# A hybrid encoder layer on one core: a new order of instructions and a new assignment of buffers, which count on the landing of stores

## The chip, the cores and the metric

One core of a Trainium2 chip runs the whole layer in one launch. The time is in device microseconds, the median of three runs. The engines are named as in the profile: PE (TensorE matmuls) and PEld (its weight loads), DVE (VectorE), ACT (ScalarE), POOL (GpSimd) and SP (SyncE, which here only issues DMAs).

## The reference

One layer on 512 tokens of width 1024, in f32:

```
h = rmsnorm(x) ; p = h @ w_in                      # 1024 -> 9248 columns
rx, ry, qkv, z, ba, gates = split(p)
y_rnn = rglru(conv4(rx), gelu(ry)) @ w_rnn_proj    # 12 blocks of 128, forward and backward scan
y_dn  = deltanet(silu(conv4(qkv)), z, ba) @ w_dn_proj   # 8 heads, chunks of 64, two directions
x = x + (sigmoid(g1) * y_rnn + sigmoid(g2) * y_dn) @ w_out
gt, up = split(rmsnorm(x) @ w_gate_up)             # 1024 -> 2 x 2816
x = x + (silu(gt) * up) @ w_down
out = rmsnorm(x)
```

## The kernel before

Large products are made in three parts: each f32 operand is split into a rounded fp32r part (`hi`, an ACT cast) and the rest (`lo`, a DVE subtraction), and PE adds hi·hi, hi·lo and lo·hi, 128x512 or 128x256 at a time. Most of the large products are also done with seven block products in place of eight (`merged`, `products`, `gate_up`, `down_first`, `down_second`), whose sums of weight blocks are made ahead of time. The small products (transposes, the deltanet's 128x128 state, its triangular inverse) are plain f32.

The program runs in this order: the norm and transposition of x; four groups of rglru blocks (`rg_group`), with the first deltanet front (`dn_front`) and the z product (`zset`) between; the rnn projection (`rset`); for each of four pairs of heads `dn_mats`, `dn_inverse`, `dn_state`, `dn_out`, interleaved with the next front and with steps of the two gate products; the deltanet and output projections; the FFN. Weights come by SP's DMA queue, mostly 512 KB to a transfer; some are added up in place by POOL's.

Five intermediate results go out to DRAM and come back, and the stores lie on SP's queue like the loads: `gcr` (the deltanet's cumulated decays; it comes back broadcast to all partitions in `dn_mats`), `xqd` (sums of blocks of the normalized x), `zs` (silu of z), `osums` (sums of blocks of w_out, stored by `out_sums`, 512 KB to a store, two stores for each of four j) and `sums` (the same for w_down). `kept` is a small sixth.

No statement of the kernel runs where it is written. Each engine call is recorded (`Rec`), and `Plan.emit` (lines 491 to 511) issues the 9344 recorded calls in the order of a table of numbers, `ORDER`. A second table, `HOMES`, gives each of 1930 tiles of the groups `t2` (2 KB a partition), `t4` (4 KB a partition) and `ps` (a PSUM bank) the number of the buffer it lives in. Every line of the profile is L525 for that reason, and the tile names carry the meaning: `t4788` is the 788th tile, from group `t4`. Both tables come out of a planner that is not part of the kernel. What the chip must wait for is added when the calls are issued: `emit` has the first writer of a reused buffer wait for its last users on other engines,

```
for other, last in before[home].items():
    if other != eng:
        self.tc.add_manual_dep(ins, last.name, info, reason="the buffer's last use")
```

and a load by SP into a buffer that an SP store is reading waits besides for the landing of that store, although both are on one queue: a DMA only reads its source after it was issued. That wait stands in the built program whatever the planner thinks of it. SP takes its instructions in order, so whatever stands behind a waiting load waits with it.

Each DMA of SP and ACT reports its landing on one of eight semaphores, DMAHW0 to DMAHW7, taken in turn. A DMA therefore also waits for the landing of the one that had its semaphore before it, eight DMAs back (in the rows below: the one DMAHW that goes up by one from row to row).

Of the kernel before, what the change touches and what calls it, by code (L numbers as in the profile page):

```python
# [31 lines left out]
11 0 2 1685 1686 10 14 3 5 7 1 151 152 154 70 9 1703 12 13 140 1687 153 1689 143 1688 1690 65 17 18 19 20 21 22 23  # L32
24 25 26 27 34 36 28 29 30 15 16 35 33 31 32 41 44 42 37 39 43 38 45 66 1697 1691 1692 47 1704 1723 1698 51 49 50 71
1705 1706 53 67 68 72 40 73 1707 1708 59 74 1741 1724 57 1693 1694 1699 1700 1701 1695 77 234 1742 97 96 158 52 69
46 1696 1702 58 75 54 55 78 56 76 1725 1726 48 79 80 81 89 1727 1728 1743 1744 88 60 93 63 64 1715 1709 84 61 82
1716 1717 1718 1710 62 90 85 1729 1735 83 1719 1720 1745 1746 1711 1712 1713 1714 1736 1737 1730 1738 1739 1740 92
1731 1732 1733 1734 1747 1748 1753 1754 104 99 1749 1755 1721 105 106 100 1756 107 1750 1751 135 109 133 1752 98 159
160 1757 101 86 119 117 102 103 1758 1722 116 108 91 94 126 134 125 87 127 132 95 312 390 155 1763 110 313 235 144
118 111 112 236 124 130 113 314 122 161 1759 120 128 138 162 163 164 165 166 167 168 169 170 171 172 315 316 139 237
238 239 317 318 319 320 240 241 242 243 244 245 246 247 248 249 250 251 252 253 254 255 256 257 258 259 260 261 262  # L40
321 322 323 363 364 324 325 326 327 328 329 330 331 332 333 334 136 335 129 336 131 114 1764 123 121 137 263 115 6
337 338 339 340 341 342 343 344 345 346 365 264 265 266 267 268 269 270 271 272 273 173 1760 753 347 1111 1080 1081
1762 754 756 174 175 1112 1113 176 177 757 391 178 147 142 141 146 157 145 149 216 274 275 276 277 179 156 762 278
279 280 180 181 182 183 184 148 185 767 150 418 186 187 188 189 190 191 281 282 283 284 192 348 349 350 351 352 3931
609 353 354 355 356 357 358 359 360 286 855 285 287 856 909 5682 289 193 361 288 362 196 665 666 417 582 636 857 290
392 1761 203 195 197 367 194 528 291 1235 198 368 419 583 292 369 293 199 637 370 1766 910 294 371 393 638 394 395
396 397 398 399 400 401 402 403 404 405 406 407 408 409 410 411 412 413 414 415 416 200 366 529 204 421 205 206 372
422 303 1173 858 859 8 207 423 4804 304 299 208 295 296 297 298 4805 305 306 860 861 862 474 424 425 300 301 530 381
373 374 307 308 210 302 863 375 426 309 310 211 584 531 532 533 376 311 780 209 420 427 385 386 387 388 1765 475
1236 777 534 212 779 435 436 377 378 379 380 864 865 866 867 868 869 870 871 382 383 882 883 1021 213 778 214 781  # L50
786 791 439 440 441 872 873 874 875 876 877 878 879 880 881 431 432 215 433 384 389 758 760 442 434 796 218 535 428
429 536 768 770 437 763 585 430 886 438 782 759 219 448 1114 610 1115 586 764 1116 449 476 587 443 787 588 887 537
538 539 540 1117 541 542 543 544 545 546 1118 1119 765 1237 1120 453 884 547 788 548 549 755 888 783 1174 589 590
591 592 593 594 595 596 597 598 599 600 601 451 992 550 551 766 602 603 445 552 553 554 667 559 792 889 890 604 605
606 607 608 444 560 772 1121 1122 784 1175 761 502 790 1083 1084 1085 1086 1087 1088 1123 1124 1125 1126 1127 1128
1129 1130 1131 1132 1133 1134 1135 1136 1082 789 911 1089 1090 556 501 455 896 1137 785 561 450 885 562 1091 1092
1093 1094 1095 1096 904 769 771 1097 1098 1099 1100 1101 1102 1103 891 452 454 1104 1105 468 469 892 613 614 1106
797 799 477 462 463 1022 1023 478 479 480 481 482 905 900 901 893 902 897 898 483 484 485 486 487 488 489 490 491
492 493 494 495 496 456 615 616 1107 1108 1138 611 612 1142 903 617 894 464 1024 1025 828 555 899 794 793 795 912
497 498 499 500 895 906 557 1109 563 1110 1238 1239 1240 1241 1242 1243 564 465 913 558 505 506 1026 907 937 908  # L60
1139 773 775 936 565 566 774 776 1244 1140 507 1027 1028 1141 618 470 508 1055 1057 446 503 1029 1030 1031 1032 1033
1034 1245 1246 1247 1248 1249 1250 914 1035 1036 915 1054 1056 1251 1252 1253 1254 1255 1256 1257 1258 1259 1260
1261 4896 1037 1038 1039 1040 577 578 801 447 457 1041 569 1042 993 471 573 1266 1043 1044 1045 1046 472 619 620 621
570 571 574 575 1068 1069 509 802 567 568 916 917 918 919 920 921 201 1047 922 923 924 925 1070 504 926 1262 927 928
929 930 931 932 933 934 576 579 935 511 515 510 512 963 513 572 1176 1177 1072 938 622 516 1178 517 514 1263 580 518
940 829 466 723 1143 631 623 632 633 804 805 806 807 202 1071 994 1073 634 624 625 626 627 628 629 630 467 1179 1180
1181 1182 1183 1184 1185 1186 995 725 458 1279 941 1187 731 724 808 809 1188 1189 810 581 728 732 1190 1191 1192
1193 1194 1195 811 812 1196 1197 1373 1198 1199 1264 942 939 803 813 814 815 816 817 818 819 820 821 822 459 823 824
830 1200 825 831 826 730 827 996 997 998 999 1000 1001 1002 964 943 944 950 954 832 1003 1004 1204 217 1005 1006
1007 1008 1009 1010 1011 1012 1013 1014 1015 1201 1265 946 1202 1016 1282 833 1017 1018 733 727 729 945 947 951 952  # L70
955 948 956 726 734 834 635 1203 668 669 670 671 672 673 460 674 675 676 677 678 679 473 741 747 680 1205 835 958
959 960 836 735 4822 681 682 683 684 742 953 685 686 949 687 688 689 690 957 639 694 640 519 641 520 691 521 642 643
1283 1145 1146 961 798 800 748 523 524 525 644 645 1147 1286 461 646 647 648 649 650 522 850 651 695 652 653 654
1148 655 656 657 1149 743 749 744 751 745 736 1150 1151 658 659 660 661 662 1152 962 1319 526 842 1269 527 4861 837
843 844 851 852 1374 1019 846 847 848 692 1207 1048 228 227 663 1320 750 1281 4823 746 737 853 752 1144 1208 1209
1210 1211 1212 1213 1214 1215 1216 1217 1218 1219 1220 838 839 840 4789 1206 1375 738 229 1321 965 4824 4825 230
2374 849 1059 1221 1222 1223 1224 1225 1226 1227 1228 1229 1230 1153 1154 1155 1156 1157 1158 1159 1160 841 845 739
1061 1231 1232 664 4806 1051 1053 4856 4807 1427 1058 1233 1060 854 231 693 1050 1052 2393 232 1272 1234 966 967 968
969 970 1271 1161 1162 1163 1164 1165 1166 1167 1168 2367 1169 2400 1454 1062 1270 1074 4 2394 1170 1171 1376 1377
1378 1379 1380 1381 1382 1383 1384 1385 1386 1387 1388 1389 1390 1391 971 972 1273 1063 1280 1284 1392 1393 1394  # L80
1395 1268 1075 1396 1397 1398 1399 220 233 1428 973 974 975 976 977 978 979 980 981 982 983 984 985 1274 1172 1267
1400 1401 1076 1077 1285 223 1287 1078 1346 1064 4839 696 1296 1404 1298 4838 4860 1275 1276 1277 1278 1300 1405
1406 1049 1290 224 2397 1402 2395 1656 2368 2371 2372 2375 2401 986 2370 2379 2378 1322 2369 987 988 4857 1407 1408
1065 1020 1323 1324 1325 1326 2382 989 2377 221 222 1327 1328 1329 1330 1331 1332 1333 1334 1335 1336 1337 1338 1339
1340 1341 1342 1343 1344 1345 1350 1351 1352 1353 1066 1067 1657 1409 740 4788 2376 1455 4790 2380 2373 225 1403
1288 697 698 699 700 4840 990 701 702 703 704 705 706 707 708 709 710 711 712 713 1297 1301 1429 714 1430 1347 1289
1291 1293 1294 1295 1292 991 715 716 717 718 719 720 721 1658 4791 1305 1431 1432 1433 1456 722 1418 1419 1354 1422
1299 1303 1348 1302 2917 1306 2381 2387 4928 1420 1423 1424 1425 1355 1457 1349 4874 1421 1426 2365 2386 2384 2385
1410 2366 1411 1412 1414 1415 1416 1417 1413 1434 1435 1436 1437 1438 1439 1440 1441 1442 1443 1444 1445 1573 1446
# [1925 lines left out]
```

## Time and profile before

| | us |
|---|---|
| median of 3 runs (lowest, highest) | 1043.67 (1043.47, 1044.1) |
| the profiled execution, its own time | 1040.58 |
| its span, first to last instruction | 1038.9 |
| PE busy in the span | 1022.7 |
| DVE busy | 946.1 |
| ACT busy | 749.8 |
| POOL busy | 121.1 |

The profiled execution is 3.09 us faster than the median of the timed runs. In the rows that follow, a busy time is the time in which the engine had at least one instruction under way; on PE the ends of matmuls are modelled and overlap, so a matmul's price is the distance from its start to the next one's. "x" counts instructions. In a row of the waits, the engine that waited stands ahead of the arrow and what released it behind.

### The profile page before, as it was taken

The page shows a single profiled execution, that of the slowest core. Times are in us where ns is not written, and L with a number is a line of the kernel's source. Part 1 is how long each engine was busy: PE and PEld are TensorE (multiplying, and loading weights), DVE is VectorE, ACT ScalarE, POOL GpSimd, SP SyncE. Part 2 cuts the span into 40 slices and gives each one's busy share as a digit, 9 for nine tenths or more (in the row PEclk, how much of TensorE's full clock was granted, in tenths as well). Part 3 has the DMA queues.
Part 4 walks back from the last instruction along what each step waited for, and adds up shares of the span by engine and source line. Part 5 has one row for each costly group of instructions (what it writes and reads, how often), then busy time and mean ns, then how long its engine had stood idle before and what let it go on. Part 6 is the DMA issues. An engine that isn't in the chain of part 4 may idle for free. (4 is left out here: it accounts for less than half of the span.)

```text
span 1038.9 us, 18186 instructions
## 1 busy us (share of the span) xinstructions
PE 1022.7 (98%) x6623; PEld 888.7 (86%) x6623; DVE 946.1 (91%) x1707; ACT 749.8 (72%) x1384; POOL 121.1 (12%) x165
## 2 busy tenths in 40 slices
PE   9999999999999998999999999999999999999997
PEld 8888888888888886879878888889999999998886
DVE  6999999998778888979999988999999899999997
ACT  7899999986674577798887585778454555556664
POOL 6000001220012216221322000000000000000000
PEclk9999999999999999999999999999999999999999
DMA  9954236796678789995966745961575643155632
GB/s 301 272 162 132 67 100 185 181 248 166 177 199 185 168 243 284 222 264 172 260 138 154 216 123 186 289 174 62 173 224 173 207 149 102 42 160 191 236 103 82
DMA packets 170873, 186.30 MB, mean 179 GB/s; under 512 B 8704, under 2 KB 120464, under 8 KB 170784
## 3 DMA queue, kind: packets, MB, share of 16 engines
q1 hardware_dynamic: 157648, 156.43, 48.5%
q0 software_dynamic: 11808, 25.30, 14.4%
q10 hardware_dynamic: 1328, 3.42, 0.9%
q8 instruction: 52, 0.85, 0.3%
q14 instruction: 37, 0.30, 0.1%
HBM read 159.92 MB, written 18.91 MB: 172 GB/s over the span
## 5 line engine op out<-in xcount | busy, mean ns | idle before, releaser
L525 DVE TENSOR_TENSOR t<-t,t 128x1024 fp32r<-128x1024 f32 (+14 forms) x839 | 550.7, 685 | 37.4 <-ACT t L525 17.8
L525 PE MATMUL ps<-t,t 128*128 128x512 f32 (+3 forms) x3195 | 574.9, 328 | 5.3 <-DVE t L525 2.3
L525 PEld LDWEIGHTS ps<-t,t 128*128 128x128 f32 (+1 forms) x3195 | 454.8, 180 | 70.8 <-DVE t L525 4.4
L525 ACT CAST t<-t 128x1024 fp32r<-128x1024 f32 (+2 forms) x418 | 323.2, 808 | 128.6 <-PE ps L525 64.0
L525 PE MATMUL ps<-hh,t 128*128 128x512 f32 (+2 forms) x1424 | 369.7, 340 | 0.3 <-ACT t L525 0.3
L525 PEld LDWEIGHTS ps<-hh,t 128*128 128x128 f32 (+1 forms) x1424 | 247.1, 189 | 29.5 <-ACT t L525 0.7
L525 PE MATMUL ps<-hl,t 128*128 128x512 f32 (+2 forms) x720 | 230.7, 339 | 0.0
L525 PEld LDWEIGHTS ps<-hl,t 128*128 128x128 f32 (+1 forms) x720 | 134.4, 189 | 14.3
L525 ACT COPY t<-ps 128x256 f32<-128x256 f32 (+3 forms) x168 | 69.9, 434 | 62.4 <-PE ps L525 53.1
L525 ACT ACTIVATE t<-t 128x128 f32<-128x128 f32 (+5 forms) x118 | 71.8, 618 | 19.0 <-DVE t L525 14.7
L525 DVE SCALAR_TENSOR_TENSOR t<-ps,par,t 128x511 f32<-128x511 f32 (+1 forms) x108 | 79.0, 745 | 6.8 <-ACT t L525 5.8
L525 ACT ACT_TABLE_LOAD x56 | 71.8, 1283 | 4.4 <-issue 1.9
L525 DVE TENSOR_TENSOR t<-ps,t 128x256 f32<-128x256 f32 (+1 forms) x102 | 53.3, 528 | 8.4 <-PE ps L525 5.7
L525 DVE TENSOR_TENSOR t<-t 128x512 f32<-128x512 f32 (+1 forms) x84 | 53.4, 643 | 2.8 <-PE ps L525 2.3
L525 PEld LDWEIGHTS ps<-t,na 128*128 128x128 f32 (+2 forms) x640 | 43.7, 146 | 7.4 <-issue 3.2
L525 PE MATMUL ps<-t,na 128*128 128x128 f32 (+2 forms) x640 | 49.0, 233 | 0.9 <-DVE t L525 0.6
L525 ACT ACTIVATE t<-ps,par 128x512 f32<-128x512 f32 x68 | 45.4, 707 | 4.2 <-PE ps L525 3.9
L525 POOL TENSOR_SCALAR_AFFINE_SELECT t<-t 128x512 f32<-128x512 f32 x32 | 25.9, 864 | 184.8 <-ACT t L525 153.9
L525 PE MATMUL ps<-ident,t 128*128 128x128 f32 (+1 forms) x232 | 44.5, 274 | 1.2 <-ACT t L525 0.5
L525 POOL DMA_DIRECT2D t<-in_w_in_dram x24 | 31.1, 1364 | 73.4 <-DVE t L525 39.6
L525 PEld LDWEIGHTS ps<-ident,t 128*128 128x128 f32 (+1 forms) x232 | 29.2, 141 | 7.9 <-ACT t L525 1.5
L525 ACT ACTIVATE t<-ps 128x256 f32<-128x256 f32 (+1 forms) x46 | 21.8, 486 | 16.3 <-PE ps L525 15.9
(153 smaller groups left out, 683.5 us busy)
## 6 DMA issues: line engine op xcount, KB each, us to landing
t<-in_w_in_dram SPq DMA_DIRECT2D x66, 512.0 KB, 5.4
t<-in_w_gate_up_dram SPq DMA_DIRECT2D x44, 512.0 KB, 4.7
t<-xqd SPq DMA_DIRECT2D x48, 256.0 KB, 4.9
t<-in_w_in_dram POOLq DMA_DIRECT2D x24, 512.0 KB, 7.5
t<-in_w_down_dram SPq DMA_DIRECT2D x22, 512.0 KB, 4.4
t<-in_w_down_dram SPq DMA_DIRECT2D x33, 256.0 KB, 4.1
t<-in_w_in_dram SPq DMA_DIRECT2D x24, 256.0 KB, 4.2
t<-in_w_out_dram SPq DMA_DIRECT2D x12, 512.0 KB, 5.3
```

What stands on the lines that cost most here:

```text
L525: self.plan.ops.append((self.eng, {x.tensor.name for x in aps}, outs, lambda: real(*a, **kw)))
```

## The change

Nearly all of `ORDER` and of `HOMES` is new: 1788 of the 1930 buffer numbers differ, and a call stands on average 28 places (of 9344) from where it stood, at most 702. The code, the operations, their shapes and the DMAs are the same; only what the engines do next, and where tiles lie, is changed. The planner that wrote the tables counts a wait that it had not counted: a load into a buffer that a store of the same queue reads waits for that store's landing. The core of the diff:

```
 ORDER = """
-11 0 2 1685 1686 10 14 3 5 7 1 151 152 154 70 9 1703 12 13 140 1687 153 1689 143 1688 1690 65 17 18 19 20 21 22 23
...
+11 0 2 1685 1686 10 14 1 3 5 7 151 140 152 153 154 70 143 1687 1688 1689 1690 65 17 18 19 20 21 22 23 24 25 36 26 27
...
 HOMES = """
-1 3 0 4 2 0 4 9 5 15 1 3 6 7 6 7 2 8 9 2 10 11 14 12 13 13 12 25 23 15 22 20 6 3 7 1 5 0 14 24 5 12 7 5 5 0 5 0 10 2
...
+1 5 0 7 2 0 3 8 4 13 1 3 6 7 4 6 3 8 9 0 10 11 12 13 14 18 17 27 24 15 26 23 6 5 1 3 2 2 19 25 7 9 1 14 0 10 0 6 12
...
```

What that does is seen in the instructions of an engine in their order. The first place is SP's queue in `out_sums` and `dn_mats` of the second pair of heads, in the profile of before at 382 to 394 us. `osums<-t4911` and `osums<-t4910` are the two stores of one j; `t4788` and `t4784` receive the broadcast decays; `t4476` is a block of gate weights. Before:

```order
L525 DMA osums912_989<-t4911_988 128x1024 [waits DMAHW4_49,DVE_49]
L525 DMA t4788_865<-gcr100_177 128x4x128 [waits DMAHW4_49,DMAHW5_49,DVE_49,PE_49]
L525 DMA t4784_861<-gcr100_177 128x4x128 [waits DMAHW6_49,PE_49]
L525 DMA osums912_989<-t4910_987 128x1024 [waits DMAHW7_49,DVE_49]
L525 DMA t4476_553<-in_w_in_dram 128x2x512 [waits DMAHW7_49,DMAHW0_49]
L525 DMA t4471_548<-in_w_in_dram 128x2x512 [waits DMAHW1_49,DMASW5_49,DVE_49]
L525 DMA t4488_565<-in_w_in_dram 128x2x512 [waits DMAHW2_49,DMASW7_49,PE_49]
```

After:

```order
L525 DMA osums912_989<-t4911_988 128x1024 [waits DMAHW2_49,DVE_49]
L525 DMA t2475_552<-xqd112_189 128x512 [waits DMAHW3_49,PE_49]
L525 DMA osums912_989<-t4910_987 128x1024 [waits DMAHW7_49,DMAHW4_49,DVE_49]
L525 DMA t4788_865<-gcr100_177 128x4x128 [waits DMAHW5_49,DMASW2_49,DVE_49]
L525 DMA t4784_861<-gcr100_177 128x4x128 [waits DMAHW6_49,PE_49]
L525 DMA t4476_553<-in_w_in_dram 128x2x512 [waits PE_49]
L525 DMA t2474_551<-xqd112_189 128x512 [waits DMAHW0_49]
L525 DMA t4865_942<-in_w_in_dram 128x8x128 [waits DMAHW1_49,PE_49]
```

Before, the store of `t4911` reports on DMAHW4 and the next load waits for DMAHW4, because `t4788` lies in the buffer of `t4911`; the store of `t4910` reports on DMAHW7 and the load of `t4476`, into the buffer of `t4910`, waits for it. After, the four tiles lie elsewhere, and no row behind the two stores (they report on DMAHW2 and DMAHW4) waits for them.

Over the whole queue: of the seven loads or stores behind an `osums` store that waited for its landing within three rows, one is left (`t4608`, a block of w_rnn_proj, behind the store of `t4922`); of the loads that wait for the landing of a `sums` store at most three rows ahead there were two, and there are three.

The second place is PE at the start, where the transposes of the second half of x (`ident`, f32) meet the first z products (fp32r, into ps458 and ps459). Before:

```order
L525 MATMUL ps458_535<-t4464_541,t424_101 128x512
L525 MATMUL ps65_142<-ident1_78,t457_134 128x128
L525 MATMUL ps62_139<-ident1_78,t457_134 128x128
L525 MATMUL ps65_142<-ident1_78,t457_134 128x128
L525 MATMUL ps458_535<-t4464_541,t424_101 128x512
L525 MATMUL ps459_536<-t4464_541,t424_101 128x512
L525 MATMUL ps63_140<-ident1_78,t457_134 128x128 x2
L525 MATMUL ps459_536<-t4464_541,t424_101 128x512
L525 MATMUL ps63_140<-ident1_78,t450_127 128x128
```

After:

```order
L525 MATMUL ps459_536<-t4464_541,t424_101 128x512 x2
L525 MATMUL ps64_141<-ident1_78,t457_134 128x128
L525 MATMUL ps65_142<-ident1_78,t457_134 128x128
L525 MATMUL ps62_139<-ident1_78,t457_134 128x128
L525 MATMUL ps63_140<-ident1_78,t457_134 128x128
L525 MATMUL ps62_139<-ident1_78,t457_134 128x128
L525 MATMUL ps65_142<-ident1_78,t457_134 128x128
L525 MATMUL ps63_140<-ident1_78,t457_134 128x128
L525 MATMUL ps64_141<-ident1_78,t457_134 128x128
```

The f32 transposes stand together, where before PE went back to fp32r twice among them. Over the whole order PE goes from an f32 matmul to an fp32r matmul 169 times before and 158 times after. ACT's order has 61 table loads where it had 56; every other instruction is there as often as before.

876 rows, old and new, of tables (HOMES, ORDER) are left out of this document.

## Prediction

> **What bounds the kernel now.** I read the page's shares first, then a table of stages, then PE's waits, then SP's, and last the two places where PE stood still longest.
>
> The page's first line for PE:
>
> ```profile
> PE 1022.7 (98%) x6623; PEld 888.7 (86%) x6623; DVE 946.1 (91%) x1707; ACT 749.8 (72%) x1384; POOL 121.1 (12%) x165
> ```
>
> PE is without work for 1038.9 - 1022.7 = 16.2 us of the span, and the change leaves each of its matmuls in place. Where those 16.2 us lie is seen in the stretches of time (length, then busy time and count of PE, PEld, DVE, ACT and POOL, PE's clock, share of the DMA engines, GB/s):
>
> ```profile
> 0.00:52.00 52.00, 49.39 (x301) 43.39 (x302) 42.12 (x89) 43.94 (x81) 17.57 (x29) 1.00 0.99 286
> 52.00:160.00 108.00, 108.00 (x480) 88.64 (x481) 106.03 (x132) 105.05 (x148) 0.00 (x0) 1.00 0.39 120
> 160.00:385.00 225.00, 225.00 (x1278) 187.07 (x1276) 192.16 (x314) 163.37 (x273) 42.80 (x48) 1.00 0.79 196
> 385.00:415.00 30.00, 26.73 (x122) 20.92 (x120) 26.06 (x45) 21.30 (x60) 16.73 (x24) 1.00 0.88 258
> 415.00:530.00 115.00, 114.70 (x792) 95.07 (x791) 103.50 (x262) 98.81 (x214) 28.42 (x40) 1.00 0.85 213
> 530.00:545.00 15.00, 13.33 (x256) 9.89 (x255) 14.67 (x24) 12.62 (x26) 6.20 (x7) 1.00 0.87 198
> 545.00:700.00 155.00, 153.27 (x1045) 130.47 (x1046) 143.48 (x329) 109.54 (x223) 9.36 (x19) 1.00 0.66 191
> 700.00:1020.00 320.00, 319.88 (x2301) 303.12 (x2300) 304.88 (x489) 187.17 (x345) 0.00 (x0) 1.00 0.47 148
> 1020.00:1038.90 18.90, 12.35 (x61) 10.11 (x59) 13.22 (x31) 7.99 (x20) 0.00 (x0) 0.93 0.31 112
> ```
>
> PE's idle time by stage is length less busy: 2.61 at the start, 0.00 from 52 to 385, 3.27 in the thirty microseconds from 385, then 0.30, 1.67, 1.73, 0.12, and 6.55 at the end. Start and end are the first loads and the last norm, whose rows stand nearly as they did. So a new order can win at most 3.27 + 0.30 + 1.67 + 1.73 + 0.12 = 7.1 us there, 0.7%, and 3.27 of it lies in one place.
>
> The place is where SP waits for stores. SP's own waits for the landing of a store (total, times, longest):
>
> ```profile
> SPq L525 <- DMA osums<-t: 31.8, 7, 7.2
> SPq L525 <- DMA xqd<-t: 5.8, 3, 3.7
> SPq L525 <- DMA zs<-t: 5.8, 2, 5.1
> SPq L525 <- DMA sums<-t: 4.1, 2, 2.7
> ```
>
> That is 47.5 us in which nothing else went out on that queue. Most of it cost PE nothing, as the stages without idle time show. From 380 to 394 two stores follow each other; SP's issues there:
>
> ```profile
> 382.64 0.32 SPq L525 DMA_DIRECT2D osums<-t  x1
> 386.28 0.92 SPq L525 DMA_DIRECT2D t<-gcr  x2
> 387.30 0.45 SPq L525 DMA_DIRECT2D osums<-t  x1
> 392.66 1.91 SPq L525 DMA_DIRECT2D t<-in_w_in_dram  x4
> ```
>
> and its waits for stores in that window:
>
> ```profile
> SPq L525 <- DMA osums<-t: 8.0, 2, 4.8
> ```
>
> The gcr loads go out 3.64 us after the first store and the four w_in loads 5.36 us after the second, 8.0 us of it waiting. Meanwhile the DMA engines run dry and are then flooded, in 40 slices of 0.75 us from 385 to 415 (tenths of busy share, then GB/s):
>
> ```profile
> DMA  3004689840055999999999999999999999999999
> GB/s 126 0 0 147 151 222 358 323 175 22 0 41 137 350 410 404 399 393 327 293 339 388 382 265 210 238 254 262 270 265 256 225 197 259 334 379 378 393 423 333
> ```
>
> What hangs on those loads, in order of time (start, length, in brackets the idle time before and its releaser):
>
> ```profile
> 390.71 4.00 POOL L525 TENSOR_SCALAR_AFFINE_SELECT t<-t 128x512 f32<-128x512 f32 x4 [3.43 <-DVE t L525]
> 391.38 2.04 ACT L525 ACTIVATE t<-t,ngc 128x128 f32<-128x128 f32 x6 [2.74 <-POOL t L525]
> 397.28 1.22 POOL L525 DMA_DIRECT2D t<-in_w_in_dram  x1 [2.57 <-DVE na L525]
> 398.02 1.14 POOL L525 TENSOR_SCALAR_AFFINE_SELECT t<-t 128x512 f32<-128x512 f32 x1
> 399.20 0.88 DVE L525 SCALAR_TENSOR_TENSOR na<-ps,dns,t 128x256 f32<-128x256 f32 x2 [2.03 <-POOL t L525]
> 402.65 0.96 PE L525 MATMUL ps<-t,t 128*128 128x512 f32 x3 [2.06 <-DVE t L525]
> 411.55 1.05 ACT L525 CAST t<-t 128x1024 fp32r<-128x1024 f32 x1 [1.85 <-DMA t<-in_w_in_dram]
> 413.73 0.50 PE L525 MATMUL ps<-t,t 128*128 128x512 f32 x1 [1.19 <-ACT ps L525]
> ```
>
> And the landings of the gcr loads from 385 to 415 (count, size, median us from issue):
>
> ```profile
> t<-gcr SPq DMA_DIRECT2D x2, 256.0 KB, 4.4
> ```
>
> 386.28 + 4.4 is 390.7, the moment at which POOL starts: POOL masks the decays that gcr brought, ACT takes their exp, POOL masks again, and only then can DVE write `na`; its 2.03 us of waiting pass on to PE as 2.06. Then ACT stands 1.85 us for a w_in load and PE 1.19 for ACT. I read both of PE's waits, 2.06 + 1.19 = 3.25 of the 3.27, as the late tail of these two stores.
>
> **The change part by part.**
>
> *Stores waited for.* The order shows that neither the gcr loads nor the w_in loads behind these stores wait for them any more. Removed are up to 3.64 and 5.36 us of SP. What that is worth to PE is bounded above by the stage's idle time, 3.27, and by what DVE has to spare there, 30.00 - 26.06 = 3.94; below by nothing (a loss is the second rival). I take 3.27, since the chain leads from the store to both waits without a break. What is late next is the ordinary run of the neighbouring stages: from 415 to 700 PE is idle 0.30 + 1.67 + 1.73 = 3.70 us in 285, so 0.4 in 30. Net -2.9. The other osums, xqd, zs and sums waits count nothing: PE's own work hides them, and if that cover went they would cost what the covered places do not cost now.
>
> [...]
>
> *Fewer changes of precision on PE.* Of the 169 places where PE goes from f32 to fp32r, 11 are gone. Their price:
>
> ```profile
> 405.19 0.48 PE L525 MATMUL ps<-hh,t 128*128 128x512 f32 x1
> 405.51 0.39 PE L525 MATMUL ps<-hl,t 128*128 128x512 f32 x1
> 405.74 0.40 PE L525 MATMUL ps<-hh,t 128*128 128x512 f32 x1
> ```
>
> The first comes straight behind transposes and takes 405.51 - 405.19 = 0.32 us to the next start; the second takes 0.23. So 0.09 each, 11 x 0.09 = 1.0 us, on PE itself and hence on the path. Its bounds are 0 (four of the 11 are at the start, where PE waits for loads anyway) and 1.0; I take -1.0, as the rest of PE's time has no holes to hide it.
>
> *Five more table loads on ACT.* Each as on the page:
>
> ```profile
> L525 ACT ACT_TABLE_LOAD x56 | 71.8, 1283 | 4.4 <-issue 1.9
> ```
>
> 5 x 1.28 = 6.4 us on ACT. By the order the surplus lies where the rnn projection and the first deltanet stage run, around 210 to 320 us:
>
> ```profile
> 208.00:320.00 112.00, 112.00 (x700) 91.84 (x699) 92.19 (x158) 77.47 (x109) 15.75 (x21) 1.00 0.77 194
> ```
>
> ACT has 112.00 - 77.47 = 34.5 us free there, which hides 6.4; without that cover the price would be the whole 6.4. I take 0.
>
> *Everything else moved.* 28 places on average is a few microseconds, for every engine and for the POOL queue's DMAs too. That makes new waits at places that I cannot see. Below: nothing, since 52 to 385 shows that an order without any is possible. Above: as much as the worst place of before, 3.27. What is there to go by are PE's waits between 530 and 700 (total, times, longest), which no store explains:
>
> ```profile
> PE ps L525 <- ACT t L525: 1.0, 3, 0.6
> PE ps L525 <- DVE t L525: 0.9, 3, 0.4
> PE ps L525 <- issue: 0.8, 1, 0.8
> PE ps L525 <- DVE so L525: 0.3, 1, 0.3
> ```
>
> I add one wait as long as the longest of these, +0.8; the ones already there I expect again, as the same chains (inverse, state) stand in the same places.
>
> Sum: -2.9 - 1.0 + 0 + 0.8 = -3.1 us. Against the profiled execution that is 1040.58 - 3.1 = 1037.5; the median of the timed runs stands 3.09 above the profiled one, so 1043.67 - 3.1 = 1040.6.
>
> **The rivals.** A measurement of this kernel can tell about 0.2% from no change, 2.1 us: faster means under 1041.6, slower over 1045.8.
>
> *Earlier, but no sooner there.* The loads leave SP up to 5 us earlier and land when they did, since the engines are full, or another late thing (POOL's queue, held 2.57 us for DVE just ahead of 398) ends at the same moment. For it: shares of 9 from 395 on. Against it: the dry slices. Time: only the other terms are left, -1.0 + 0.8, so 1043.5.
>
> *Loads nearer to their use (slower).* In exchange for the free queue the order lets loads go later. Pricing the PE rows between a load's last issue and its first reader at 0.23 us for 512 columns and half for 256, 62 of 312 loads have less than 6 us where 53 had, and from the middle of the rnn projection to the deltanet stage (240 to 360 us of PE work) the mean lead falls from 21 to 17 us. The landings of w_rnn_proj from 385 to 415:
>
> ```profile
> t<-in_w_rnn_proj_dram SPq DMA_DIRECT2D x3, 512.0 KB, 8.4
> ```
>
> A w_rnn_proj load that now has 3.4 us of lead would be 5 us late at 8.4. I price such a place by the old one, 3.27 us of PE. One new place cancels the gain (-2.9 - 1.0 + 0.8 + 3.27 = +0.2, 1043.8); from two on the kernel is slower: +3.4, 1047.1. Against it: 160 to 385 shows no idle PE at all with landings of the same kind.
>
> *More than the store places.* If the new order also takes the waits between 530 and 700, 1.67 + 1.73, the time is 1040.6 - 3.4 = 1037.2. For it only that all was planned anew; against it that DVE is busy 14.67 of 15.00 us there.
>
> *The change does not do what it says.* One osums wait and three sums waits are left, and a planner's rule can be met on paper only. The order speaks against it at the dearest place; elsewhere the waits cost nothing either way, so the time would be that of the first rival.
>
> **How the numbers follow.** The forecast 42%; more than the store places 6%; earlier but no sooner 26%, and not what it says 6%, both no change; loads nearer to their use 20%. Faster is then 0.48, no change 0.32, slower 0.20. The predicted time is 1040.6. The range must reach the high rival's 1047.1 and the low one's 1037.2; with a little for the spread of the runs, 0.6 us, I give 1036.8 to 1047.2. The forecast's unknown terms at their ends (new waits 0 to 3.27, PE's changes of precision 0 to 1.0) make 1039.8 to 1044.0; where they pass 1041.6 I have counted it as no change.
>
> **What would show each step.** In the profile after: SP's waits for osums fall from 31.8 us to one of about 5; the 30 us that hold the second pair's `dn_mats` have PE idle under 1 us and no DVE wait for POOL of 2 us; the engines show no empty slices between two stores; PE's busy time is about 1 us less; ACT's table loads are 61 and PE does not wait for ACT between 210 and 320. I am wrong if PE's waits of that stage stay with the loads out early (then the landing, not the issue, held it), or if PE shows idle time between 160 and 385, where it had none.

## The result, and the profile after

The new tables make the kernel faster: median 1036.74 us (four runs, 1036.35 to 1039.43) against 1043.88 for the kernel before (four runs), ratio 0.9935, 95% interval 0.9916 to 0.9954. Three later comparisons of the same two kernels, set out below, gave 0.9963 (0.9943 to 0.9982), 0.9949 (0.9929 to 0.9968) and 0.9946 (0.9932 to 0.9959). The middle of the four, 0.9948, is 5.4 us of 1043.5; the forecast was 3.1. The prediction's range was 1036.8 to 1047.2: this first median lies 0.06 us below it, its ratio applied to the prediction's 1043.67 gives 1036.9, and the later medians are 1038.87, 1037.72 and 1038.05. Single executions scatter: by 6 us for the kernel before (1041.1 to 1046.9), by 8 us for the changed one (1035.5 to 1043.5).

The profiled execution of the changed kernel took 1039.43 us, 2.7 more than its median, and that of before 1040.58, 3.1 less than its median. So the two pages differ by 1.2 us only, and a gain of 5 can't be read from this pair alone. What they do show is where things stand. PE's line of the page:

```profile
PE 1023.9 (99%) x6623; PEld 888.8 (86%) x6623; DVE 948.6 (91%) x1707; ACT 755.6 (73%) x1389; POOL 128.6 (12%) x165
```

The stages after (columns as in the prediction; stages are cut by time; counted matmul by matmul, PE is within 2 us of the same point of its work):

```profile
160.00:385.00 225.00, 225.00 (x1276) 187.00 (x1274) 194.11 (x313) 168.19 (x278) 47.77 (x47) 1.00 0.78 197
385.00:415.00 30.00, 29.66 (x137) 23.78 (x136) 28.97 (x50) 23.10 (x63) 17.05 (x25) 1.00 0.99 281
415.00:530.00 115.00, 112.83 (x781) 93.34 (x780) 103.00 (x261) 98.17 (x211) 29.72 (x40) 1.00 0.84 221
530.00:545.00 15.00, 14.12 (x269) 10.96 (x268) 14.69 (x24) 14.21 (x32) 6.56 (x7) 1.00 0.74 152
545.00:700.00 155.00, 153.78 (x1042) 130.90 (x1041) 143.53 (x330) 107.73 (x221) 9.47 (x19) 0.99 0.61 181
700.00:1020.00 320.00, 320.00 (x2303) 303.65 (x2302) 305.94 (x489) 188.54 (x346) 0.00 (x0) 1.00 0.49 153
```

PE's idle time from 385 to 415 is 0.34 us where it was 3.27, and from 530 to 545 0.88 where it was 1.67; from 415 to 530 it is 2.17 where it was 0.30. From 160 to 385 there is still none. SP's waits for DMAs after (total, times, longest):

```profile
SPq L525 <- DMA t<-t: 21.2, 3, 8.3
...
SPq L525 <- DMA osums<-t: 8.0, 1, 8.0
SPq L525 <- DMA sums<-t: 6.4, 2, 4.4
...
SPq L525 <- DMA kept<-t: 1.9, 1, 1.9
```

The wait for `osums` has fallen from 31.8 us, seven times, to the one that the order had left. Of the three waits for POOL's adding DMAs (`t<-t`, 21.2 us in all), two are new. SP's issues at the two stores, and the DMA engines from 381 to 411 (40 slices of 0.75 us):

```profile
381.99 0.34 SPq L525 DMA_DIRECT2D osums<-t  x1
382.90 0.33 SPq L525 DMA_DIRECT2D t<-xqd  x1
383.44 0.33 SPq L525 DMA_DIRECT2D osums<-t  x1
385.89 1.06 SPq L525 DMA_DIRECT2D t<-gcr  x2
387.51 0.37 SPq L525 DMA_DIRECT2D t<-in_w_in_dram  x1
```

```profile
DMA  5945879996897999999999999999999999669999
```

PE reaches the same matmul about 1.6 us later here than in the profile of before. Counted from PE's work, the gcr loads go out 386.28 - 385.89 + 1.6 = 2.0 us sooner and the first w_in load 392.66 - 387.51 + 1.6 = 6.8 us sooner. The lowest slice is 4, where before there were two stretches at 0.

### The profile page after: what moved, and what is told of

The parts are those of the page before. It is cut to its first block, busy times and chain, and to the rows that moved or that the text cites. A ratio compares the mean times of both kernels' runs of the same rounds, so it can differ in the third digit from the quotient of the medians.

```text
span 1037.7 us, 18160 instructions
## 1 busy us (share of the span) xinstructions
PE 1023.9 (99%) x6623; PEld 888.8 (86%) x6623; DVE 948.6 (91%) x1707; ACT 755.6 (73%) x1389; POOL 128.6 (12%) x165
## 5 line engine op out<-in xcount | busy, mean ns | idle before, releaser
L525 DVE TENSOR_TENSOR t<-t,t 128x512 fp32r<-128x512 f32 (+14 forms) x839 | 551.5, 686 | 40.6 <-ACT t L525 16.8
L525 ACT CAST t<-t 128x512 fp32r<-128x512 f32 (+2 forms) x418 | 323.3, 809 | 118.0 <-PE ps L525 42.4
L525 PE MATMUL ps<-hh,t 128*128 128x512 f32 (+2 forms) x1424 | 373.6, 340 | 0.1
L525 POOL TENSOR_SCALAR_AFFINE_SELECT t<-t 128x512 f32<-128x512 f32 x32 | 29.6, 1029 | 196.8 <-DMA t<-gcr 180.2
L525 PE MATMUL ps<-ident,t 128*128 128x128 f32 (+2 forms) x232 | 43.6, 273 | 1.3 <-ACT ps L525 0.6
L525 PEld LDWEIGHTS ps<-ident,t 128*128 128x128 f32 (+2 forms) x232 | 29.0, 141 | 8.6 <-ACT t L525 1.3
L525 POOL TENSOR_SCALAR t<-t,dnse 128x128 f32<-128x128 f32 x48 | 29.8, 711 | 43.3 <-PE ps L525 29.0
```

The costliest lines, as they stand in the source:

```text
L525: self.plan.ops.append((self.eng, {x.tensor.name for x in aps}, outs, lambda: real(*a, **kw)))
```

## The experiments

All ratios are to the kernel before, run on the same chip beside it; "us" is the ratio's distance from 1 times 1043.5.

| kernel | ratio (95%) | us |
|---|---|---|
| before_again | 0.9999 (0.9988 to 1.0010) | -0.1 |
| after_again, a_third, a_fourth | 0.9963, 0.9949, 0.9946 | -3.9, -5.3, -5.6 |
| b_one_pair | 0.9961 (0.9949 to 0.9974) | -4.1 |
| b_all_stores | 0.9964 (0.9950 to 0.9978) | -3.8 |
| b_first | 0.9978 (0.9962 to 0.9993) | -2.3 |
| b_second | 0.9996 (0.9976 to 1.0015) | -0.4 |
| a_back | 0.9978 (0.9964 to 0.9993) | -2.3 |
| b_dve | 0.9993 (0.9981 to 1.0005) | -0.7 |
| b_both | 0.9967 (0.9949 to 0.9985) | -3.4 |

**Both kernels again, and the store place alone.** The two theories: the gain comes from the one place of two stores (the prediction), or from the order elsewhere. In b_one_pair the order and the buffers are those of before; the two stores of j = 0 read another tile, so nothing has to wait for them (the sums of w_out for that j are left out of the result):

```
-        Q.dma_start(osums[j][:, 0], s_)
-        Q.dma_start(osums[j][:, 1], rb)
+        src = (f(hh)[:, 0:2, :], f(hh)[:, 2:4, :]) if j in (0,) else (s_, rb)
+        Q.dma_start(osums[j][:, 0], src[0])
+        Q.dma_start(osums[j][:, 1], src[1])
```

b_all_stores has `j in (0, 1, 2, 3)`.

> The kernel before once more, for a second profiled execution and for the noise: its first profiled execution was 3 us faster than its timed runs, so the profile may lack what the timed runs lose. Every theory: ratio 1.000 within 0.002. If the stage of 385 to 415 us is what costs, its PE busy time is again about 3 us under the length of the stage, and where the execution is 3 us longer than the first one, the extra idle time of PE shows in one stage.

> The changed kernel once more, for a second profiled execution: the first was 2.7 us slower than its timed runs. Every theory: ratio to the kernel before 0.9935 within 0.002. If the store place was what the change won, the 30 us from 385 show PE idle under 1 us again; the other 4 us of the gain must show as less idle time of PE, or as shorter matmuls, in some other stage.

> The order and buffers of before, but the two stores of osums912 (t4911 and t4910, the ones at 382 and 387 us) send the same number of bytes out of hh, so that nothing waits for their landing; the output's w_out product is wrong for that j. Store place theory: SP's 8.0 us of waiting there are gone, PE's 2.06 and 1.19 us too, and the time falls by 2.9 us (ratio 0.997). If the place costs more in a typical execution than in the one profiled: by up to 7 us (0.993). Rival, the full engines hold the loads anyway or the gain comes from the order elsewhere: within 1 us (0.999 to 1.001).

> As the one before, for all eight osums stores: of SP's 47.5 us of waiting for stores 31.8 go. The forecast gave the other places nothing, since PE is busy all through there: the same time as with the one pair freed, within 0.5 us. Rival, the other places cost too in a typical execution: 1 us or more below the one pair, towards the 7 us of the whole change.

after_again came out at 0.9963, slower than the 0.9915 to 0.9955 expected; its seven executions spread from 1036.0 to 1043.5 us. Freeing the one pair gives 4.1 us (2.7 to 5.3), as much as the whole change gave beside it (3.9). The 2.9 forecast lies inside that interval. Freeing all eight stores gives no more. The stage in b_one_pair:

```profile
385.00:415.00 30.00, 29.99 (x139) 24.23 (x138) 29.01 (x52) 24.56 (x64) 18.38 (x26) 1.00 1.04 302
```

PE's idle time there is 0.01 us. If the pair is worth more than the 3.27 that was idle, which the interval leaves open, the second profile of the kernel before shows a reason: first PE's wait at that place and then two stretches with PE's clock (the third column from the right, 1.00 at full speed):

```profile
397.51 4.84 PE L525 MATMUL ps<-t,t 128*128 128x512 f32 x13 [2.19 <-ACT t L525]
```

```profile
395.00:405.00 10.00, 7.82 (x29) 5.92 (x28) 6.49 (x13) 6.95 (x15) 6.50 (x10) 0.83 0.93 278
530.00:545.00 15.00, 13.41 (x226) 10.66 (x224) 14.42 (x26) 11.61 (x25) 6.19 (x7) 0.90 0.78 184
```

Behind the 2.19 us of waiting the clock was lower for a while: 0.83 over 10 us is 3.4 us at 0.50 (an estimate with the clock of the tail's stretches in the last section), a loss of 1.7 beside the idle time. The run "tail" below, the same kernel up to its end, has the same 0.83 there. The execution on which the prediction was built had no such stretch while PE worked (1.00 in all its stages up to 1020), and was 3 us faster than the median.

**The waits put back, and the two stores one by one.** In a_back the changed kernel waits again; the second store (call 3930) stands behind the gcr load (3173) as it did before:

```
+STORES = {3173: (3929,), 1786: (3930,)}
...
             ins = run().ins
+            seen[i] = ins
+            for store in STORES.get(i, ()):
+                self.tc.add_manual_dep(ins, seen[store].name, info, reason="the store's landing")
```

b_first and b_second are b_one_pair with one of the two lines.

> The changed kernel a third time, as the yardstick for the next ones and for a third profiled execution. By the seven executions of the second time (ratio 0.9963, 0.9943 to 0.9982) and the four of the first (0.9935): 0.9935 to 0.997. If it is the store place alone that it won, it is no faster than before with that one pair of stores freed (0.9961); below 0.994 something else in the order is worth 2 us or more.

> The changed kernel with the waits of that one place put back: the gcr load t4788 waits for the landing of the store of t4911, the second store goes behind that load as in the order before, and the w_in load t4476 waits for the landing of the store of t4910. Store place theory: the wait for the second store holds the w_in loads some 4.5 us longer, PE stands again for 1 to 3 us around 395 to 415, ratio to the kernel before 0.997 to 0.9995, that is 1 to 3 us slower than the changed kernel. The first wait may cost nothing here, since the gcr loads already go out 2 us after the second store for PE's sake. Rival, the gain lies in the order elsewhere: no slower than the changed kernel, ratio 0.994 to 0.9965.

> The kernel before with only the first of the two stores (of t4911) freed, so that the gcr loads don't wait for its landing; the w_in loads still wait for the second store's. By the prediction's chain (gcr, POOL's mask, ACT's exp, DVE's na, PE) this takes PE's 2.06 us: 2 us less, ratio 0.998. Rival, the two waits add to one stall and the second is what counts: 0.999 to 1.000.

> The kernel before with only the second store (of t4910) freed: the w_in loads go out some 5 us sooner, the gcr loads as before. By the prediction's chain this takes the 1.19 us that PE waits for ACT's cast of w_in: 1.2 us less, ratio 0.9989. Rival, the w_in loads are what fed the late POOL and ACT work too: most of the 3.8 us that both stores together gave, ratio 0.997 or less.

In a_back's profile the waits are there again, three where the changed kernel had one, and PE's idle time from 385 to 415 is 2.25 us:

```profile
SPq L527 <- DMA osums<-t: 14.7, 3, 7.2
```

They cost 0.9978 - 0.9949 = 0.0029, 3.0 us, when put back into the new order; from the scatter of the two sets of executions I estimate 0.7 to 5.4. The first store alone is worth 2.3 us (0.7 to 4.0), so the chain over gcr, POOL's masks and `na` costs, as the prediction read it. The second comes out at 0.4, with an interval from a gain of 2.5 to a loss of 1.6; two of its twelve executions took 1048.8 and 1050.0 us, and its median is 1.6 under that of the kernel before. So the second's forecast 1.2 is neither shown nor excluded, and which of the two is dearer isn't shown.

**The third pair's inverse, and what a change of precision costs.** The profiles of the first eight runs pointed to a second place. The third pair's `dn_inverse` runs 32x32 and then 64x64 matmuls. Before, from the first of the 32x32 group to the last 64x64 group:

```profile
532.57 0.38 PE L525 MATMUL ps<-t,na 32*32 32x32 f32 x12
...
541.67 1.20 PE L525 MATMUL ps<-na,t 64*64 64x64 f32 x32
```

and after:

```profile
532.95 0.87 PE L525 MATMUL ps<-t,na 32*32 32x32 f32 x64
...
540.51 1.32 PE L525 MATMUL ps<-na,t 64*64 64x64 f32 x32 [0.38 <-ACT na L525]
```

That is 9.10 us before and 7.56 after, for the same matmuls but one of 8 columns. In the other profiles of the old order it is 9.06 to 10.55, in those of the new one 7.55 or 7.56. Part of what holds the inverse up before is one call on DVE, in the profile of before beside POOL's masks:

```profile
535.26 0.74 DVE L525 SCALAR_TENSOR_TENSOR t<-ps,par,t 128x510 f32<-128x510 f32 x1
535.91 2.10 DVE L525 SCALAR_TENSOR_TENSOR t<-t,so,t 128x128 f32<-128x128 f32 x1
```

```profile
535.48 3.01 POOL L525 TENSOR_SCALAR_AFFINE_SELECT t<-t 128x512 f32<-128x512 f32 x4
```

```profile
L525 DVE SCALAR_TENSOR_TENSOR t<-t,so,t x32: 341/346/2102, 520.0 to 639.1; 128x128 f32<-128x128 f32 x32
```

Of 32 such calls (the last row: shortest, median, longest in ns) one takes 2102 in place of 346, the one that starts inside POOL's select. The call ahead of it, with one operand in PSUM, overlaps POOL's select too and takes 0.74 us, like its group (a mean of 0.745 on the page). In the new order none of the 32 takes over 0.353 us, and another call is long while POOL's select runs (535.34 to 539.00):

```profile
536.68 1.25 DVE L525 TENSOR_TENSOR so<-so,nq 128x8 f32<-128x8 f32 x1
```

The median of the twelve such calls in that profile is 0.16 us. Why these two are long beside a select and the call with an operand in PSUM isn't was not tried. In b_dve the call that took 2.10 us (2787) goes behind the five that feed the inverse and two more; in b_both the store place is mended by hand besides, by moves of four loads and six exchanged buffers (exchanged to the end of the program, so that 137 of the 1930 numbers differ):

```
 b_dve, ORDER, the calls on DVE (place: call)
 4491: 4597
-4498: 2787
 4500: 4598
...
 4567: 4630
 4570: 3099
 4572: 3101
+      2787
 4573: 2786
 b_both besides, ORDER and HOMES (place before -> after; buffer before -> after)
 load of t4788   3040 -> 3052   7 -> 3
 load of t4784   3053 -> 3056   3 -> 17
 load of t4476   3066 -> 3079   2 -> 5
 load of t4471   3091 -> 3099   5 -> 9
 t4618           3058           17 -> 7
 t4619           3107           9 -> 2
```

The kernel "tail" is the kernel before with a test behind its end:

```
+    for rep in range(3):
+        for i in range(48): turn(pz[:, 0:P], ident); round_mm()
+        for i in range(48): turn(pz[:, 0:P], ident)
+        for i in range(48): round_mm()
+    for rep in range(4):
+        for n in (1, 2, 3, 4):
+            for i in range(44): round_mm()
+            A.activation(gr, po, AF.Copy)
+            for i in range(n - 1): A.activation(gr, gr, AF.Copy)
+            T.matmul(pz[:, 0:P], gr[:, 0:P], ident, start=True, stop=True)
```

> The changed kernel a fourth time, as the yardstick on this chip: 0.9935, 0.9963 and 0.9949 so far, so 0.9935 to 0.9965 whatever the theory. In its profile PE is idle again for 1 us or more somewhere between 410 and 520 us, where before had 0.3 to 0.8, and the stretch of the third pair's inverse (around 530 to 540) is 1.5 us shorter than in the order before.

> The kernel before with one DVE call moved: the product t4667<-t4667,so,t4699 (128x128), which takes 2.10 us in place of 0.35 in every profile of that order because it runs beside POOL's affine selects, goes behind the five DVE calls that feed the third pair's inverse. Theory that the rest of the gain comes from this inverse: PE's wait of 1.2 to 1.5 us there shrinks to 0.3, the time falls by 1 to 1.5 us, ratio 0.9985 to 0.999; if a half-speed stretch of PE's clock behind that wait goes too, up to 2.5 us, 0.9975. Rival, another step of the inverse is late in its place: 0.9995 to 1.0005.

> The kernel before with that DVE call moved and with the store place mended by hand: four loads (t4788, t4784, t4476, t4471) stand 12, 3, 13 and 8 places later and six buffers are exchanged, so that no load there waits for a store's landing; all other calls stand as before, and nothing of the computation is left out. If the two places make up the gain of the whole new order: 3.8 + 1.3 = 5.1 us, ratio 0.995, the same as the changed kernel within 0.001. If the new order gives 1 to 2 us back elsewhere (410 to 520 us), this one is as much faster than the changed kernel: 0.993 to 0.994. If the four loads come too late where they stand now, or ACT waits for the first store in their place: 0.997 or more.

> The kernel before, with calls on PE and ACT added behind its end that have no part in the result. First, three times, 48 pairs of one f32 transpose and one 128x512 fp32r matmul in turn, then 48 transposes and 48 matmuls each together. By the prediction's 0.09 us for a change from f32 to fp32r the mixed run takes 48 x 0.09 = 4.3 us longer than the two plain ones; if the 0.09 was the matmul's own late start and not a price, under 1 us. Then, four times, 44 matmuls (10 us) and a pause in which PE waits for 1, 2, 3 and 4 ACT calls (about 0.9, 1.5, 2.1 and 2.7 us): theory that PE's clock is halved for 3.41 us when too much of one stretch of 3.41 us was idle: half-speed rows behind the longer pauses, not behind every one, none behind the shortest. Rival, a pause must fill a whole such stretch: none at all.

b_dve: the inverse in its profile:

```profile
534.98 0.38 PE L523 MATMUL ps<-t,na 32*32 32x32 f32 x12
...
543.32 1.20 PE L523 MATMUL ps<-na,t 64*64 64x64 f32 x32 [0.49 <-ACT t L523]
```

8.34 us, so this call is 0.8 of the 1.5; no call of its group takes over 0.354 us any more, so the 2.10 us came with its old place. The time falls by 0.7 us, with an interval from a gain of 2.0 to a loss of 0.5, so a gain in time isn't shown. The other half lies in how the new order places the rest of the inverse and was not tried alone.

b_both missed the 5.1 us expected: 3.4 us (1.6 to 5.3), no more than the one pair alone gave. In its profile, an execution of 1042.78 us where the median was 1039.26, the mended place is not mended:

```profile
385.00:415.00 30.00, 25.82 (x116) 19.79 (x115) 23.58 (x46) 18.68 (x50) 10.38 (x17) 1.00 0.90 254
```

```profile
406.64 1.04 ACT L523 CAST t<-t 128x1024 fp32r<-128x1024 f32 x1 [4.19 <-DMA t<-in_w_in_dram]
```

No load waits for a store there any more, but ACT stands 4.19 us for a w_in load. One slow execution doesn't show how often that comes, and which of the four later places did it was not tried.

a_fourth is as fast as expected, and its profile shows what the new order gives back. DVE first, then PE, then two stretches:

```profile
420.10 3.53 DVE L525 TENSOR_TENSOR t<-t,t 128x1024 fp32r<-128x1024 f32 x10 [3.98 <-DMA osums<-t]
```

```profile
421.38 3.11 PE L525 MATMUL ps<-t,t 128*128 128x512 f32 x7 [2.19 <-DVE t L525]
```

```profile
415.00:425.00 10.00, 7.81 (x29) 6.00 (x28) 5.57 (x20) 7.06 (x12) 0.88 (x1) 0.83 0.82 200
415.00:530.00 115.00, 112.16 (x769) 92.37 (x768) 99.87 (x256) 97.34 (x210) 26.10 (x37) 0.99 0.82 215
```

It is a wait for a store's landing again, but now DVE waits: it writes into a buffer that an `osums` store (issued at 408.83) is still reading. All five profiles of the new order have such waits of DVE, 3.2 to 7.5 us in all, and at this place they cost PE over 2 us in two of them; of the six old-order profiles with only the stores' source changed or nothing, none has one. In both of the two a stretch at a lower clock follows (0.83 above; 0.83 from 425 to 435 in a_third).

In the tail, the second of the three rounds (PE; the mixed part runs from 1073.33 to 1089.80, then 48 transposes, then 48 matmuls):

```profile
1073.33 0.27 PE L527 MATMUL ps<-ident 128*128 128x128 f32 x1
1073.35 0.47 PE L527 MATMUL ps<-t 128*128 128x512 f32 x1
1073.66 0.27 PE L527 MATMUL ps<-ident 128*128 128x128 f32 x1
...
1089.80 5.40 PE L527 MATMUL ps<-ident 128*128 128x128 f32 x48
1094.96 11.18 PE L527 MATMUL ps<-t 128*128 128x512 f32 x48
1105.97 0.27 PE L527 MATMUL ps<-ident 128*128 128x128 f32 x1
```

From start to start, 48 pairs in turn take 1089.80 - 1073.33 = 16.47 us; 48 transposes and 48 matmuls apart take 5.16 and 11.01, 16.17 together. 0.30 in 48 changes is 0.006 us each, where the prediction had 0.09.

And the pauses (in brackets the pause, in the row behind it the 44 matmuls that follow):

```profile
1161.46 0.49 PE L527 MATMUL ps<-ident,t 128*128 128x128 f32 x2 [1.41 <-ACT t L527]
1161.70 10.26 PE L527 MATMUL ps<-t 128*128 128x512 f32 x44
1174.03 0.49 PE L527 MATMUL ps<-ident,t 128*128 128x128 f32 x2 [2.07 <-ACT t L527]
1174.28 10.25 PE L527 MATMUL ps<-t 128*128 128x512 f32 x44
...
1222.97 0.49 PE L527 MATMUL ps<-ident,t 128*128 128x128 f32 x2 [2.07 <-ACT t L527]
1223.21 11.86 PE L527 MATMUL ps<-t 128*128 128x512 f32 x44
```

Behind the eight pauses of 0.75 and 1.41 us no matmul was slow; behind three of four of 2.07 and two of four of 2.73 the next ones were: 11.47 to 11.87 us for 44 in place of 10.25. The price is 1.2 to 1.6 us.

## Why the prediction was right or wrong

The direction was right. The sum was -3.1, the runs give about -5.4. The forecast's own terms at their ends gave 1039.8 to 1044.0, and all four medians of the changed kernel lie below that; the stated range reaches down to them only because it was drawn out to a rival that had 6%, and the first median lies at its very edge (by the prediction's own 0.6 under the rival's 1037.2 the range would begin at 1036.6, not at 1036.8).

*Stores waited for, -2.9.* The mechanism is shown, from both sides: -4.1 when taken away, +3.0 when put back. Every sign named for it came: one `osums` wait left (of 8.0 us, not about 5), PE idle for 0.34 us in the 30, no 2 us wait of DVE for POOL, no empty slices of the engines. The size was probably short, because the price was the idle time of one lucky execution: a wait of 2 us on PE is followed in part of the executions by a stretch at a lower clock (0.83 over 10 us in before_again, none in before; in the tail 3.40 us at 0.50, 1.2 to 1.6 us more). The interval of -4.1 (2.7 to 5.3) holds 2.9, so that it was short isn't shown.

*Other stores, nothing.* Right: eight stores freed give what two do.

*Fewer changes of precision, -1.0.* Wrong. The step that failed is the price. A matmul behind a transpose starts 0.02 us after it (1073.35 behind 1073.33), early, and so its distance to the next start is long; the pair pays 0.006 us. Eleven are 0.07 us. The sign named for it, PE's busy time 1 us less, can't be read from the page (1023.9 for 1022.7): the execution after has one stretch at half clock between 604 and 612 (0.69 and 0.89 over 4 us each, 0.50 from 605.6 to 608.8), a loss of 1.7 us, and that of before has none while PE works. Two without one, after_again and a_back, have 1021.1 and 1022.7. The -1.0 stood, by luck, where gains lay that the sum did not have.

*Five more table loads on ACT, 0.* Right. The page after has

```profile
L525 ACT ACT_TABLE_LOAD x61 | 78.3, 1283 | 9.2 <-DVE t L525 6.0
```

and PE is busy for all of 160 to 385.

*New waits, +0.8.* Right in kind, too small: from 415 to 530 PE's idle time grows from 0.30 to 2.17 in the first profile after and to 115.00 - 112.16 = 2.84 in the fourth, 1.9 to 2.5 us more. The bound of 3.27 holds for the idle time.

*The rivals.* "More than the store places" had 6% and is in part what happened: the third inverse is 1.5 us shorter in the traces. The reason given against it was that DVE is busy 14.67 of 15.00 us there. That busy time holds 2.10 - 0.35 = 1.75 us of one call beside POOL's select, which another place of the call took away in b_dve. "Earlier but no sooner there" falls with b_one_pair, "loads nearer to their use" with PE's 225.00 of 225.00; "doesn't do what it says" is true only of what the prediction did not look at, the waits of DVE.

*The start, nothing.* The prediction took its rows to stand nearly as they did. PE is idle for 2.5 to 2.6 us from 0 to 52 in the six profiles of the old order, and for 1.4 to 2.7 in the five of the new one, on average 0.7 less. The second profile after:

```profile
0.00:52.00 52.00, 50.48 (x306) 43.90 (x307) 43.14 (x89) 44.80 (x83) 18.16 (x29) 1.00 1.00 286
```

Added up, -4.1 - 0.1 - 1.5 + 2.2 - 0.7 = -4.2, against a measured 3.9 to 6.8. This is a rough sum: the first term is a difference of times, the others are read from traces, and that the inverse and the start are worth their share in time no run shows. The clock doesn't settle the rest. From 530 to 545 it was granted below 1 in four of six profiles of the old order (0.89 or 0.90) and in none of five of the new one, but from 604 to 616 in two of the six and in three of the five (over 600 to 612: 0.81 in b_first; 0.86, 0.89 and 0.75 in the first, third and fourth of the new order).

## What to carry to other kernels

A wait for a store's landing belongs to whoever next touches the buffer, an engine as well as a queue: count it for loads alone and it comes back on DVE, here with 3.2 to 7.5 us. Price a stall from several executions, since one profile shows its idle time but not always the lower clock behind it (1.00 in before, 0.83 in before_again). And before you call an engine full, look for its instructions that take a multiple of their group's median, here 2.10 us for 0.35.

## What the runs showed of the hardware

PE's clock in the tail, one execution, was halved in stretches of one length (length, PE's busy time and count, PE's clock, DMA share, GB/s; the last row is a stretch that stayed at full speed):

```profile
1223.80:1227.20 3.40, 3.40 (x10) 0.50 0.00 0
1237.40:1240.80 3.40, 3.00 (x8) 0.50 0.00 0
1275.00:1278.40 3.40, 3.40 (x9) 0.50 0.00 0
1326.20:1329.60 3.40, 3.40 (x10) 0.50 0.00 0
1339.80:1343.20 3.40, 2.85 (x8) 0.50 0.00 0
1172.60:1176.00 3.40, 1.97 (x10) 1.00 0.02 5
```

They begin 13.6, 37.6, 51.2 and 13.6 us apart, 4, 11, 15 and 4 times 3.41: in this execution all five lie on one grid of 3.41 us. On it a pause was followed by half clock or not by how it fell. The pause of 2.07 that ended at 1222.97 lies within one slot (1220.4 to 1223.8) and the next slot is slow; that which ended at 1174.03 is cut by the grid at 1172.6 into 0.6 and 1.4, and nothing happens. The longest part in one slot that did nothing is 1.7 us (a pause of 2.73, 1184.52 to 1187.25, cut at 1186.25), the shortest that did something 2.07. Where between the two the border lies, and whether the grid is the same in other executions, was not tried.
